# Making the four weight sums of a gate and up block in DRAM, by adding transfers issued from GpSimd

## The chip, the cores and the metric

The kernel runs on one core of one Trainium2 chip. Its five engines work at the same time and wait for each other through semaphores: TensorE (in the profile PE for its matmuls, PEld for its weight loads), VectorE (DVE), ScalarE (ACT), GpSimd (POOL) and SyncE (SP). SP here does nothing but issue transfers (DMAs); ACT issues a few; before the change GpSimd issues none. Each engine takes its instructions strictly in the order of the program, so one that waits holds up all that stand behind it on that engine. The metric is the device time of one execution in microseconds (us); lower is better.

## The reference

One layer of an encoder block on 1024 tokens of width 1024, in float32. The first half makes a convolution group and a neighbourhood attention group and adds their projection to the input. The second half, which the change touches, is a SwiGLU feed-forward network:

```python
h = rms_norm(x, norm2_g[l])
x = x + (jax.nn.silu(h @ w_gate[l]) * (h @ w_up[l])) @ w_down[l]
```

`w_gate` and `w_up` are 1024 x 2816, `w_down` is 2816 x 1024.

## The kernel before

Every float32 operand of a large product is split in two parts, `hi` (a rounded copy, made by ACT) and `lo` (the operand minus `hi`, made by DVE or GpSimd); `mac` (lines 115 to 118) then issues three matmuls, hi by hi, hi by lo and lo by hi. So each operand costs one ACT copy and one subtraction before TensorE may use it.

The core goes through these stages: input projections with the convolution beside them (to about 230 us of the span), attention (to about 340), output projection and second norm (to about 397), gate and up products (to about 800), down projection (to the end).

The gate and up product uses a scheme with seven products instead of eight. The 2816 columns of the two weights are 22 blocks `i` of 128 columns (`FB = 22`). For each block the 1024 rows are two halves, and with gate and up that gives four quadrants: `b11` and `b21` are the two halves of gate, `b12` and `b22` those of up, each 512 rows by 128 columns, 256 KB. Products `m1`, `m2` and `m3` need `b11`, `b21` and `b22` as they are. Products `m5`, `m6`, `m7` and `m4` need four sums T1 to T4 of quadrants. In the kernel before, `load_gu` (line 1071) loads a block in two transfers of 512 KB on SP into two of the four `R` buffers, and `t_sums` (line 1089) makes the four sums as differences on DVE, for two of them on GpSimd, into `ts` tiles (`tqa` for the first two blocks):

```python
l, r = ((b12, b11), (b22, lr(tsum[i, 0])[0]), (b22, b12), (b21, lr(tsum[i, 0])[1]))[n - 1]
(pool if (i, n) in ON_POOL else dve).tensor_tensor(o, l, r, OP.subtract)
```

The other side of each product is a sum of token blocks: `left` (line 1258) makes S1 to S4 from the normed activations `xT` on DVE. `evac` (line 1340) combines the accumulators of the seven products.

For blocks from 4 (`m1`) and 6 (`m2`) on, `m1` and `m2` are themselves done for two blocks at a time by the same scheme one level down (`part`, `prep_part`; tiles `q...`, `qa`, `qb`, `qc`, `qd`, `qs`), with loads of their own (`qr`).

The order is written out by hand. `products` is the list of the products in TensorE's order; `tasks` is the list of the operand preparations, each with a place some products ahead; `prep` takes tasks from it, splits (mostly on ACT and GpSimd) and asks for the next load. R buffers come free when the splits that read them are done. In the first half, `step` (line 468) is called once after each group of matmuls (some 5.5 us) and holds the vector work beside them; the four attention heads' rows are normalised by `score_norm` on GpSimd (line 764) before TensorE turns them (`flip`, line 775).

Names used below: `z` the accumulators of the input projections, `p` the turned attention rows, `e` the exponentials, `cs` a channel sum of the convolution made on GpSimd (line 359), `u` the convolution's channels, `pj` the output projection, `w01r` and the like raw weight chunks loaded on SP (line 150), `tf` the tables for the attention bias built in DRAM by many small transfers, `A`, `B` and `D` the accumulators of the gate and up products.

Of the kernel before, what the change touches and what calls it, by code (L numbers as in the profile page):

```python
# [12 lines left out]
P = 128  # L13
# [18 lines left out]
def layout(v):  # L32
    f = {k: np.asarray(a)[0] for k, a in v.items()}
    w_in = f["w_in"]
    ag = w_in[:, :2 * DC].reshape(KB, P, 8, P).transpose(2, 1, 0, 3)
    qkv = w_in[:, 2 * DC:].reshape(4, 2, P, 3, 512).transpose(3, 0, 2, 1, 4)
    gu = np.stack([f["w_gate"], f["w_up"]]).reshape(2, KB, P, FB, P).transpose(3, 0, 2, 1, 4)
# [12 lines left out]
    out = {  # L50
        "x": f["x"],
        "xp": f["x"].reshape(2, 8, 4, 16, D).transpose(4, 0, 2, 3, 1).reshape(KB, P, S),
        "xt": xt,
        "xa": np.concatenate([xt[0, 0, :, 0, :256], f["norm1_g"][:2 * P].reshape(2, P).T], axis=1),
        "ag": ag.reshape(8, P, KB * P),
        "qkv": qkv.reshape(3, 4, P, 1024),
        "wo": f["w_out"],
        "gu": gu.reshape(FB, 2, P, KB * P),
        "wd": wd,
        "rpb": f["rpb"],  # L60
        "par": par,
    }
    return {k: np.ascontiguousarray(a) for k, a in out.items()}
# [8 lines left out]
def build(ctx, tc, a):  # L72
# [201 lines left out]
    for _ in range(9):  # L274
# [5 lines left out]
    tf = {(rh, ty): dr.tile([16, 8, NH, AR[rh] * NCOL[ty]], F32, name=f"tf{rh}{ty}")  # L280
          for rh in range(2) for ty in range(3)}

    def rstd_of(ss, scale, name):
# [179 lines left out]
        nc.scalar.dma_start(vd[t * P:(t + 1) * P, :], vs)  # L463


    pend = []
# [576 lines left out]
    def square(m, h, eng=pool):  # L1043
# [4 lines left out]
        else:  # L1048
            eng.tensor_tensor(ssum[h], ssum[h], sq, OP.add)  # L1049

    def token_sums(h):
# [11 lines left out]

    def norm2(k, h):
        w = xT[k][:, h * 512:(h + 1) * 512]
        dve.scalar_tensor_tensor(w, w, g2[:, k:k + 1], rows[h], OP.mult, OP.mult)

    HK, QF = KB // 2, FB // 2
    raw_gu, top, tsum = {}, {}, {}

    def load_gu(i, j):
        if i < FB:
            raw_gu[i, j] = R(f"gu{i}{j}")
            nc.sync.dma_start(raw_gu[i, j], a["gu"][ms[i], j])
# [8 lines left out]
    ON_POOL = {("S3", 2), ("S3", 3), ("A22", 1), ("S4", 3), (3, 2), (3, 4),  # L1083
               (0, "m4"), (0, "m5"), (1, "m4"), (1, "m6")}
    ON_DVE = {(3, "m3"), (3, "m7")}

    def t_sums(i, ns):
        (b11, b21), (b12, b22) = lr(raw_gu[i, 0]), lr(raw_gu[i, 1])
        for n in ns:
            if n in (1, 3):  # L1090
                if i > 1:
                    tsum[i, n // 2] = G(f"ts{i}{n}")
                else:
                    tsum[i, n // 2] = tq_slot("tqa", 2 * i + n // 2)
            o = lr(tsum[i, (n - 1) // 2])[(n - 1) % 2]
            l, r = ((b12, b11), (b22, lr(tsum[i, 0])[0]), (b22, b12), (b21, lr(tsum[i, 0])[1]))[n - 1]
            (pool if (i, n) in ON_POOL else dve).tensor_tensor(o, l, r, OP.subtract)  # L1097


    ORDER = ("m1", "m6", "m7", "m2", "m5", "m4", "m3")  # L1100
    ms = [m + h * QF for m in range(QF) for h in range(2)]
# [23 lines left out]
    tasks.sort(key=lambda w: w[0])  # L1125
    quad, raw4, sum4 = {}, {}, {}

    def prep_part(m, i, p):
        j, o = (m, i), 512 * (m == "m2")
        if p == "load":  # L1130
            raw4[j] = G(f"qr{i}{m}")
            for b in range(2):
                nc.sync.dma_start(raw4[j][:, b * 512:(b + 1) * 512], a["gu"][ms[i + b], 0][:, o:o + 512])
            return
        w = raw4[j]
        w11, w12, w21, w22 = [w[:, o:o + 256] for o in range(0, 1024, 256)]
# [87 lines left out]
    def prep(n=1, upto=None):  # L1224
        while tasks and (n > 0 if upto is None else tasks[0][0] <= upto):
            n -= 1
            job = tasks.pop(0)[1]
            if len(job) == 3:
                prep_part(*job)
                continue  # L1230
            i, p = job
            if i > 1 and p in ("m6", "m7"):
                t_sums(i, (1, 2) if p == "m6" else (3, 4))
            b = {"m1": (0, 0), "m2": (0, 1), "m3": (1, 1)}.get(p)
            m = {"m5": 0, "m6": 1, "m7": 2, "m4": 3}.get(p)
            src = lr(raw_gu[i, b[0]])[b[1]] if b else lr(tsum[i, m // 2])[m % 2]
# [5 lines left out]
            split(*top[i, p], src, (dve,) if on_dve else (pool,))  # L1242
            if p == ("m7" if i in (2, 3) or parted(i, "m2") else "m2"):
                load_gu(i + 2, 0)
            if p == "m3":
                load_gu(i + 2, 1)


    sop = {}
# [5 lines left out]
    def left(n, k, what):  # L1255
        sub = pool if (n, k) in ON_POOL else dve
        if n not in sop:
            q = H(n, F32R).rearrange("p (w k s) -> p w k s", w=2, s=512)
            sop[n] = [[q[:, h, i] for i in range(HK)] for h in range(2)]
        o, l, r, op = {"S3": ("21", "11", "21", OP.subtract), "A22": ("22", "22", "22", None),  # L1260
                       "S2": ("22", "22", "21", OP.subtract), "S1": ("21", "22", "11", OP.add),
                       "S4": ("22", "12", "22", OP.subtract)}[n]
        if op is not None and "sum" in what:
# [17 lines left out]
        norm2(k, 0)  # L1281
        split(h2[0][:, k], h2[1][:, k], xT[k][:, :512])

    for i, j in ((0, 0), (0, 1), (1, 0), (1, 1)):
        load_gu(i, j)

    units = [(m, 0) for m in range(4, KB)] + [(m, 1) for m in range(KB)]
    for m in range(4):
        square(m, 0)
    beside = {(1, 1): [lambda: token_sums(0)], (1, 3): [lambda: token_rows(0)],  # L1290
              (0, 1): [lambda: t_sums(0, (1, 2))], (0, 3): [lambda: t_sums(0, (3, 4))],
              (2, 1): [lambda: t_sums(1, (1, 2))], (3, 1): [lambda: t_sums(1, (3, 4))]}
# [39 lines left out]

    def gate2(i, acc):
        dve.tensor_tensor(acc, acc, u2[i], OP.add)  # L1334
        act.activation(acc, acc, AF.Silu)  # L1335

    def up2(i, r, acc):
        dve.tensor_tensor(r, acc, r, OP.mult)
# [2 lines left out]
    def evac(i, p, acc):  # L1341
# [4 lines left out]
            act.copy(l, acc)  # L1346
        elif p == "m6":
            u2[i] = ST(f"u2{i}")
            dve.tensor_tensor(u2[i], acc, l, OP.add)
            if i < 2:  # L1350
                gate2(i, bank[i, "D"])
        elif p == "m2":
# [2 lines left out]
                dve.tensor_tensor(acc, acc, l, OP.add)  # L1355
            act.activation(sl[i], acc, AF.Silu)
        elif p in ("m5", "m7"):
            dve.tensor_tensor(r, acc, l if p == "m7" else r, OP.add)  # L1358
            if i < 2 and p == "m5":
                up2(i, r, bank[i, "D"])  # L1360
        elif p == "m3":
            dve.tensor_tensor(l, acc, l, OP.add)
# [115 lines left out]
    for n, (i, p) in enumerate(products):  # L1478
# [114 lines left out]

# [13 lines left out]
```

## Time and profile before

| | |
|---|---|
| median of 3 runs | 1024.64 us (1024.58 to 1025.29) |
| the profiled execution | 1025.28 us |
| its span, first to last instruction | 1023.6 us |
| granted TensorE clock | 1.000 |
| PE busy | 1017.4 us, 99% of the span |
| PEld busy | 850.2 us, 83% |
| DVE busy | 775.4 us, 76% |
| ACT busy | 480.9 us, 47% |
| POOL busy | 461.6 us, 45% |
| DMA | 151.70 MB in 75756 packets, mean 148 GB/s |

The profile has a page (busy time of each engine, the chain of work that ended last, the costliest groups of instructions, the DMA issues) and views of the trace: groups by line, waits, the timeline, and sums over chosen windows of the span. A row of a group reads: line, engine, operation, tiles written and read, shapes, count, busy time and mean time of one in ns, idle time of the engine before them and who ended it. An engine with a q is its sequencer, which waits or issues. Matmuls are pipelined: two that follow each other overlap in the records, so a busy PE says that it never lacked work, and the time between two starts is what one costs.

### The profile page before, as it was taken

To read this page: it belongs to the slowest core of one execution; us is meant where nothing else is said; L and a number is where in the kernel's file an instruction comes from. 1 tells how busy PE (TensorE), PEld (TensorE's weight loads), DVE (VectorE), ACT (ScalarE), POOL (GpSimd) and SP (SyncE) were. 2 spreads that over 40 slices of the span, in tenths; PEclk is the share of its full clock that TensorE was granted. 3 is DMA by queue.
4 is the path that set the end of the run, shared out by engine and by line. 5 is a ranking of instruction groups with operands and counts; after the bars stand their busy time and mean duration, and the time that the engine had idled before them with its cause. 6 is when DMAs were issued, how large, how long until landed. Compare 5 with 4: busy or idle time off the path is not lost.

```text
span 1023.6 us, 15128 instructions
## 1 busy us (share of the span) xinstructions
PE 1017.4 (99%) x5274; PEld 850.2 (83%) x5274; DVE 775.4 (76%) x1217; ACT 480.9 (47%) x1043; POOL 461.6 (45%) x389
## 2 busy tenths in 40 slices
PE   9999999999999999999999999999999999999998
PEld 8888888877788888888888888888888888888887
DVE  5788897896767474987787787787777766758875
ACT  7556357837878345523434343343332443433432
POOL 1036675535662356167767567567565200003200
PEclk9999999999999999999999999999999999999999
DMA  9426682236503621134334434443341696633631
GB/s 350 168 50 220 202 238 86 101 109 217 165 22 124 247 83 41 45 111 142 132 100 152 155 112 140 139 142 135 120 149 63 237 373 232 216 103 124 221 118 42
DMA packets 75756, 151.70 MB, mean 148 GB/s; under 512 B 14472, under 2 KB 23560, under 8 KB 75040
## 3 DMA queue, kind: packets, MB, share of 16 engines
q1 hardware_dynamic: 73664, 147.38, 42.7%
q10 hardware_dynamic: 2016, 3.36, 0.9%
q8 instruction: 42, 0.69, 0.3%
q14 instruction: 34, 0.28, 0.1%
HBM read 112.06 MB, written 44.11 MB: 153 GB/s over the span
## 4 chain that ended last, share of the span: by engine, by line
PE 94%; DVE 2%; ACT 2%; issue 1%; POOL 1%; DVEq 0%; POOLq 0%; ACTq 0%
PE B L116 5%; PE B L117 5%; PE B L118 5%; PE z L116 4%; PE z L118 4%; PE z L117 4%; PE D L116 4%; PE D L117 4%; PE D L118 4%; PE gl L118 3%; PE gl L117 3%; PE gl L116 3%; PE pj L116 2%; PE pj L118 2%; PE pj L117 2%; PE p L775 2%
## 5 line engine op out<-in xcount | busy, mean ns | idle before, releaser
L378 DVE SCALAR_TENSOR_TENSOR cv<-u,par,cv 128x1009 f32<-128x1009 f32 (+14 forms) x92 | 117.5, 1277 | 2.3
L1550 POOL TENSOR_TENSOR ou<-ou,resm 128x512 f32<-128x512 f32 x8 | 12.7, 1602 | 139.3 <-DVE ou L1541 126.1
L405 POOL TENSOR_TENSOR pa<-pa,pr 128x1022 f32<-128x1022 f32 (+5 forms) x24 | 58.0, 2416 | 37.3 <-ACT pr L404 33.3
L108 ACT CAST op<-sr 128x512 fp32r<-128x512 f32 x77 | 47.6, 619 | 57.5 <-PE B2d L118 26.8
L112 DVE TENSOR_TENSOR op<-sr,op 128x512 fp32r<-128x512 f32 x77 | 57.2, 742 | 17.2 <-ACT op L108 17.2
L108 ACT CAST op<-wd 128x512 fp32r<-128x512 f32 x54 | 33.4, 619 | 29.0 <-DVE wd L1445 18.1
L753 ACT ACTIVATE e<-e,mx 128x341 f32<-128x341 f32 (+5 forms) x64 | 35.3, 553 | 18.1 <-DVE mx L748 18.1
L1097 DVE TENSOR_TENSOR ts<-gu,ts 128x512 f32<-128x512 f32 x38 | 42.9, 1129 | 0.7
L764 POOL TENSOR_SCALAR e<-e,rs 128x341 f32<-128x341 f32 (+5 forms) x64 | 32.9, 528 | 22.1 <-DVE rs L762 21.6
L112 DVE TENSOR_TENSOR op<-wd,op 128x512 fp32r<-128x512 f32 x54 | 38.9, 721 | 1.7 <-ACT op L108 0.5
L748 DVE CUSTOM_DVE_ANT_0 e<-s,tab 128x341 f32<-128x341 f32 (+5 forms) x64 | 27.2, 481 | 13.1 <-PE s L731 12.9
L1049 POOL TENSOR_TENSOR sq<-sq,sq 128x512 f32<-128x512 f32 x12 | 17.0, 1418 | 41.7 <-ACT sq L1045 41.5
L1358 DVE TENSOR_TENSOR g<-D,g 128x512 f32<-128x512 f32 x22 | 15.2, 689 | 23.4 <-PE D L118 23.4
L432 ACT ACTIVATE sq<-z,r 128x64 f32<-128x64 f32 x96 | 28.2, 326 | 4.3 <-PE z L118 4.3
L1335 ACT ACTIVATE D<-D 128x512 f32<-128x512 f32 x22 | 12.8, 582 | 33.2 <-DVE D L1334 33.2
L404 ACT ACTIVATE pr<-u,par 128x1022 f32<-128x1022 f32 (+5 forms) x24 | 27.0, 1138 | 1.6 <-ACT vs L462 1.6
L116 PE MATMUL B2d<-op 128*128 128x512 f32 x66 | 25.8, 391 | 0.0
L118 PE MATMUL B2d<-op 128*128 128x512 f32 x66 | 25.7, 389 | 0.0
L117 PE MATMUL B2d<-op 128*128 128x512 f32 x66 | 25.7, 389 | 0.0
L775 PEld LDWEIGHTS p<-ident,e 128*128 128x128 f32 (+1 forms) x184 | 19.7, 135 | 6.7 <-POOL e L764 5.1
L936 DVE TENSOR_TENSOR xT<-pj,xT 128x512 f32<-128x512 f32 x16 | 10.8, 686 | 19.0 <-PE pj L118 18.8
L775 PE MATMUL p<-ident,e 128*128 128x128 f32 (+1 forms) x184 | 23.9, 277 | 0.0
(1478 smaller groups left out, 3766.2 us busy)
## 6 DMA issues: line engine op xcount, KB each, us to landing
gu<-in_gu SPq DMA_DIRECT2D x44, 512.0 KB
sr<-sd SPq DMA_DIRECT2D x77, 256.0 KB
sd<-sd SPq DMA_DIRECT2D x22, 512.0 KB
wd<-in_wd SPq DMA_DIRECT2D x36, 256.0 KB
sd<-g SPq DMA_DIRECT2D x33, 256.0 KB
x<-in_x SPq DMA_DIRECT2D x8, 512.0 KB
xT<-in_xp SPq DMA_DIRECT2D x8, 512.0 KB
xd<-xT SPq DMA_DIRECT2D x16, 256.0 KB
```

Source lines behind the costliest of these rows:

```text
L108: act.copy(hi, src)
L112: eng.tensor_tensor(*[w[..., sl] for w in (lo, src, hi.bitcast(F32))], OP.subtract)
L116: pe.matmul(acc, lh, rh, start=start, stop=False, skip_group_check=True)
L117: pe.matmul(acc, lh, rl, start=False, stop=False, skip_group_check=True)
L118: pe.matmul(acc, ll, rh, start=False, stop=stop, skip_group_check=True)
L378: dve.scalar_tensor_tensor(acc[:, o], uc[:, i], dwk[:, c, t:t + 1], acc[:, o], OP.mult, OP.add)
L405: pool.tensor_tensor(pa[:, o], pa[:, o], pr[:, o], OP.add)
L432: act.activation(sq[:, h * HD:(h + 1) * HD], z[:, h * HD:(h + 1) * HD], AF.Square, scale=r, accum_out=ss[:, h:h + 1])
L753: act.activation(e, e, AF.Exp, bias=mx.pop((i, hh)), scale=-1.0, accum_out=sums[i][:, hh:hh + 1])
L764: pool.tensor_scalar(es[i][:, hh], es[i][:, hh], rs[:, hh:hh + 1], 1.0, op0=OP.mult, op1=OP.mult)
L775: pe.transpose(pt[:m, g * P:(g + 1) * P], et[i][:, hh, k.start:k.start + m], ident)
L1097: (pool if (i, n) in ON_POOL else dve).tensor_tensor(o, l, r, OP.subtract)
```

## The change

The quadrants are laid out so that each is 32 rows of 8 KB in DRAM. For each of the 22 blocks SP copies the whole block (1 MB) from the input to a DRAM tile `td` (`copy_in`). Then four transfers issued from GpSimd, with addition, make T1, T3, T2 and T4 in place in `td` (`add_in`): T1 = b11 + b12, T3 = b12 + b22, T2 = b22 + T1, T4 = b21 + T2. That is 88 adding transfers of 256 KB. `load_gu` loads one operand of 256 KB at a time, from the input or from `td`, two of them into one R buffer, after every second split; before it loads a sum whose additions have not been issued it issues them.

Since an adding transfer can only add, the sums replace the former differences, and signs are moved to the token side: the second half of the tokens' second half of rows is normed with -g (`ng2`), `S1`, `S2` and `S3` change accordingly, `evac` subtracts where it added, and one `Silu` gets scale -1.

`add_in` is called from `step` (from its 3rd call on, between the 9th and the 21st on every other call only), after each unit of the output projection, and after every second product of the gate and up stage from the 16th on. Of the 88 additions, 30 stand in the stages before the attention loop, 12 in the output projection, 46 in the gate and up stage. The `ts` and `tqa` tiles and `t_sums` are gone; the pool of small tiles `sm` has 11 buffers instead of 12, and the scratch for GpSimd's transfer descriptors is 128 bytes of each partition instead of 64. The matmuls are the same, in the same order.

```diff
+    gu = np.stack([f["w_gate"], f["w_up"]]).reshape(2, 2, KB // 2, P, FB, P).transpose(4, 1, 0, 3, 2, 5)
+    gu = gu.reshape(FB, 4, P, 512)[:, [0, 1, 3, 2]]
...
-        return T("sm", [P, 8], 12, name)[:, :n]
+        return T("sm", [P, 8], 11, name)[:, :n]
...
+    QUAD = {"b11": 0, "b12": 1, "b22": 2, "b21": 3, "T1": 0, "T3": 1, "T2": 2, "T4": 3}
+    td = [dr.tile([P, 2048], F32, name=f"td{i}") for i in range(FB)]
+
+    def quadrant(i, q):
+        w = td[i] if q[0] == "T" else a["gu"][ms[i]]
+        return w[QUAD[q] * 32:QUAD[q] * 32 + 32]
+
+    def copy_in(i):
+        if i < FB:
+            nc.sync.dma_start(td[i], a["gu"][ms[i]])
+
+    adds = [(i, *q) for i0 in range(0, FB, 2) for q in (("T1", "b12"), ("T3", "b22"), ("T2", "T1"), ("T4", "T2"))
+            for i in (i0, i0 + 1)]
+
+    def add_in(n=1):
+        for _ in range(n):
+            if adds:
+                i, o, w = adds.pop(0)
+                if o == "T4":
+                    copy_in(i + 4)
+                nc.gpsimd.dma_start(quadrant(i, o), quadrant(i, w), accum_op=OP.add, max_dma_last_dim=8192)
...
+    ADD_AT = (3, 9, 21)
...
         behind()
+        n_step[0] += 1
+        if ADD_AT[0] <= n_step[0] and not (ADD_AT[1] <= n_step[0] < ADD_AT[2] and n_step[0] % 2):
+            add_in()
...
+    for i in range(4):
+        copy_in(i)
     take(1)
     r_rows(0)
...
+        g = ng2[:, k - 4:k - 3] if h and k > 3 else g2[:, k:k + 1]
+        dve.scalar_tensor_tensor(w, w, g, rows[h], OP.mult, OP.mult)
...
+    def load_gu():
+        if n_load[0] < len(halves):
+            w = R(f"gu{n_load[0]}")
+            for h in range(2):
+                i, p = ip = halves[n_load[0]]
+                while any((i, FACTOR[p]) == w[:2] for w in adds):
+                    add_in()
+                raw_gu[ip] = lr(w)[h]
+                nc.sync.dma_start(raw_gu[ip], quadrant(i, FACTOR[p]).rearrange("r (a m) -> (r a) m", a=4))
+                n_load[0] += 1
...
-            if i > 1 and p in ("m6", "m7"):
-                t_sums(i, (1, 2) if p == "m6" else (3, 4))
...
+            split(*top[i, p], raw_gu.pop((i, p)), (dve,) if on_dve else (pool,))
+            n_split[0] += 1
+            if n_split[0] % 2 == 0:
+                load_gu()
...
+        if n == "S2" and "sum" in what:
+            dve.scalar_tensor_tensor(block(o, k), block(l, k), -1.0, block(r, k), OP.mult, OP.subtract)
...
         proj(m, h, part_)
         unravel()
+        add_in()
...
-            dve.tensor_tensor(u2[i], acc, l, OP.add)
+            dve.tensor_tensor(u2[i], acc, l, OP.subtract)
...
+        if n > 15 and n % 2 == 0:
+            add_in()
...
-    nc = bacc.Bacc("TRN2", target_bir_lowering=False, num_devices=1, dynamic_dma_scratch_size=64)
+    nc = bacc.Bacc("TRN2", target_bir_lowering=False, num_devices=1, dynamic_dma_scratch_size=128)
```

More of the change, by code (lines that the diff above doesn't have):

```diff
@@ L281, in build @@
           for rh in range(2) for ty in range(3)}
+    QF = FB // 2
+    ms = [m + h * QF for m in range(QF) for h in range(2)]
+    QUAD = {"b11": 0, "b12": 1, "b22": 2, "b21": 3, "T1": 0, "T3": 1, "T2": 2, "T4": 3}
[15 more added lines that the diff above has]
+                nc.gpsimd.dma_start(quadrant(i, o), quadrant(i, w), accum_op=OP.add, max_dma_last_dim=8192)
     def rstd_of(ss, scale, name):
@@ L1049, in square @@
             eng.tensor_tensor(ssum[h], ssum[h], sq, OP.add)
+    ng2 = g1[:, :4]
+    dve.tensor_scalar(ng2, g2[:, 4:], -1.0, None, op0=OP.mult)
     def token_sums(h):
@@ L1065, in norm2 @@
         w = xT[k][:, h * 512:(h + 1) * 512]
[L1066 to L1074, printed above, removed]
+        g = ng2[:, k - 4:k - 3] if h and k > 3 else g2[:, k:k + 1]
+        dve.scalar_tensor_tensor(w, w, g, rows[h], OP.mult, OP.mult)
+    HK = KB // 2
+    top, raw_gu, n_split, n_load = {}, {}, [0], [0]
+    FACTOR = {"m1": "b11", "m2": "b21", "m3": "b22", "m4": "T4", "m5": "T1", "m6": "T2", "m7": "T3"}
+    def load_gu():
[8 more added lines that the diff above has]
+                n_load[0] += 1
     tqs = {}
@@ L1081, in tq_slot @@
         return tqs[name][:, q * 1024:(q + 1) * 1024]
-    ON_POOL = {("S3", 2), ("S3", 3), ("A22", 1), ("S4", 3), (3, 2), (3, 4),
+    ON_POOL = {("S3", 2), ("S3", 3), ("A22", 1), ("S4", 3),
                (0, "m4"), (0, "m5"), (1, "m4"), (1, "m6")}
     ON_DVE = {(3, "m3"), (3, "m7")}
[L1087 to L1097, printed above, removed]
     ORDER = ("m1", "m6", "m7", "m2", "m5", "m4", "m3")
-    ms = [m + h * QF for m in range(QF) for h in range(2)]
     products = [(i, p) for i0 in (0, 2) for p in ("m1", "m2") for i in (i0, i0 + 1)]
@@ L1125, in build @@
     tasks.sort(key=lambda w: w[0])
+    halves = [job for _, job in tasks if len(job) == 2]
     quad, raw4, sum4 = {}, {}, {}
     def prep_part(m, i, p):
-        j, o = (m, i), 512 * (m == "m2")
+        j = (m, i)
         if p == "load":
@@ L1132, in prep_part @@
             for b in range(2):
-                nc.sync.dma_start(raw4[j][:, b * 512:(b + 1) * 512], a["gu"][ms[i + b], 0][:, o:o + 512])
+                src = quadrant(i + b, "b11" if m == "m1" else "b21").rearrange("r (a m) -> (r a) m", a=4)
+                nc.sync.dma_start(raw4[j][:, b * 512:(b + 1) * 512], src)
             return
@@ L1259, in left @@
             sop[n] = [[q[:, h, i] for i in range(HK)] for h in range(2)]
-        o, l, r, op = {"S3": ("21", "11", "21", OP.subtract), "A22": ("22", "22", "22", None),
-                       "S2": ("22", "22", "21", OP.subtract), "S1": ("21", "22", "11", OP.add),
+        o, l, r, op = {"S3": ("21", "21", "11", OP.subtract), "A22": ("22", "22", "22", None),
+                       "S2": ("22", "22", "21", OP.subtract), "S1": ("21", "11", "22", OP.subtract),
                        "S4": ("22", "12", "22", OP.subtract)}[n]
-        if op is not None and "sum" in what:
+        if n == "S2" and "sum" in what:
+            dve.scalar_tensor_tensor(block(o, k), block(l, k), -1.0, block(r, k), OP.mult, OP.subtract)
+        elif op is not None and "sum" in what:
             dve.tensor_tensor(block(o, k), block(l, k), block(r, k), op)
@@ L1282, in h2_one @@
         split(h2[0][:, k], h2[1][:, k], xT[k][:, :512])
-    for i, j in ((0, 0), (0, 1), (1, 0), (1, 1)):
-        load_gu(i, j)
+    for _ in range(4):
+        load_gu()
     units = [(m, 0) for m in range(4, KB)] + [(m, 1) for m in range(KB)]
@@ L1357, in evac @@
         elif p in ("m5", "m7"):
-            dve.tensor_tensor(r, acc, l if p == "m7" else r, OP.add)
+            dve.tensor_tensor(r, acc, l if p == "m7" else r, OP.subtract if p == "m7" else OP.add)
             if i < 2 and p == "m5":
```

20 lines of the change are left out of this document (5 added, 15 removed).

## The prediction

> **What bounds the kernel now.** I read the page's head and chain first, then sums over the stages, then TensorE's waits.
>
> ```profile
> span 1023.6 us, 15128 instructions
> ...
> PE 1017.4 (99%) x5274; PEld 850.2 (83%) x5274; DVE 775.4 (76%) x1217; ACT 480.9 (47%) x1043; POOL 461.6 (45%) x389
> ...
> PE 94%; DVE 2%; ACT 2%; issue 1%; POOL 1%; DVEq 0%; POOLq 0%; ACTq 0%
> ```
>
> TensorE is busy in 99% of the span and carries 94% of the chain that ended last. By stage (window, its length, then busy us and count of PE, PEld, DVE, ACT, POOL, the granted clock, DMA share, GB/s):
>
> ```profile
> 0.00:230.00 230.00, 228.94 (x1043) 188.84 (x1045) 191.11 (x231) 134.21 (x350) 103.97 (x56) 1.00 0.52 169
> 230.00:340.00 110.00, 109.00 (x894) 86.20 (x893) 77.58 (x217) 86.29 (x216) 56.58 (x115) 1.00 0.45 146
> 340.00:440.00 100.00, 100.00 (x454) 82.84 (x453) 65.77 (x101) 43.43 (x75) 44.45 (x33) 1.00 0.25 90
> 440.00:525.00 85.00, 84.07 (x421) 70.91 (x420) 67.51 (x96) 30.14 (x57) 60.61 (x45) 1.00 0.34 123
> 525.00:800.00 275.00, 275.00 (x1493) 239.18 (x1492) 214.83 (x340) 98.53 (x189) 175.40 (x131) 1.00 0.38 129
> 800.00:1024.00 224.00, 220.43 (x977) 182.24 (x975) 158.60 (x237) 88.32 (x157) 20.55 (x14) 1.00 0.55 187
> ```
>
> The gate and up stage runs from about 397 to 800. TensorE is idle there for 85.00 - 84.07 = 0.93 us, all of it between 440 and 525; from 340 to 440 and from 525 to 800 it is never idle, and its clock is full. TensorE's waits between 340 and 800:
>
> ```profile
> PE q41m L118 <- POOL qb4m L112: 0.5, 1, 0.5
> PE D L116 <- DVE g L1338: 0.4, 1, 0.4
> ```
>
> So the work that the change takes away lies beside a TensorE that is full, and the change leaves the 5274 matmuls as they are. What it can win is in these two waits. What it can lose is anywhere.
>
> **What it removes from DVE and GpSimd.** 86 subtractions leave DVE and two leave GpSimd. Those of blocks 2 to 21, 78 on DVE:
>
> ```profile
> L1097 DVE TENSOR_TENSOR ts<-gu,ts 128x512 f32<-128x512 f32 x38 | 42.9, 1129 | 0.7
> L1097 DVE TENSOR_TENSOR ts<-gu 128x512 f32<-128x512 f32 x20 | 15.5, 777 | 0.0
> L1097 DVE TENSOR_TENSOR ts<-gu,gu 128x512 f32<-128x512 f32 x20 | 15.5, 774 | 0.0
> ```
>
> 42.9 + 15.5 + 15.5 = 73.9 us, and 8 more for the first two blocks at about 0.8 us, 6 us. Some 80 us of DVE go, and TensorE waited for DVE for 0.4 us in the whole stage. The worth of it is read where TensorE stops (GpSimd and one ACT row around the two waits):
>
> ```profile
> 454.86 0.68 DVE L1097 TENSOR_TENSOR ts<-gu,gu 128x512 f32<-128x512 f32 x1
> 455.00 1.68 POOL L112 TENSOR_TENSOR qb4m<-qs4m,qb4m 128x512 fp32r<-128x512 f32 x1 [5.63 <-DVE qs4m L1145]
> ...
> 462.06 1.30 POOL L1097 TENSOR_TENSOR ts<-gu,ts 128x512 f32<-128x512 f32 x1
> 462.36 0.63 ACT L108 CAST qc4m<-qs4m 128x512 fp32r<-128x512 f32 x1
> 463.32 1.30 POOL L112 TENSOR_TENSOR qc4m<-qs4m,qc4m 128x512 fp32r<-128x512 f32 x1
> 464.58 1.73 POOL L112 TENSOR_TENSOR t3m<-ts,t3m 128x512 fp32r<-128x512 f32 x1
> 464.67 0.19 PEld L118 LDWEIGHTS q42m<-qT3m,qc4m 128*128 128x128 f32 x1 [0.20 <-POOL qc4m L112]
> ```
>
> The first wait is for `qb4m`, which took 1.68 us with a `ts` of DVE beside it; `qc4m`, the same form, takes 1.30. Without that `ts` it is 0.38 us earlier. For `qc4m` TensorE's load waits 0.20 us; it starts behind a `ts` of GpSimd at 463.32, though ACT's half is there at 462.36 + 0.63 = 462.99. With the `ts` gone those 0.20 us go too, unless the addition issued there takes its place. The wait for `g` L1338 I leave as it is: DVE has its other work in front of it. Gain: 0.38 + 0.20 = 0.6 us, between 0 and 0.93. What is late next is TensorE itself. The sign changes (4 two-input sums on DVE become one form with a scalar, one tiny multiplication for -g) replace like by like, hidden by the same TensorE.
>
> **What it adds to SP.** 44 loads of 512 KB become 120 of 256 KB and 22 copies of 1 MB come: 98 issues more.
>
> ```profile
> L1074 SPq DMA_DIRECT2D gu<-in_gu x44: 327/332/1096, 338.8 to 768.4; - x44
> ...
> SPq L1074 <- DVE ts L1097: 125.5, 17, 9.8
> ```
>
> 98 x 0.33 = 33 us of issuing over 770 us, hidden, since these loads spend 125.5 us waiting for `ts` to give back its R buffer, and that wait goes. In its place SP waits for GpSimd's splits and for additions to land. Loads are asked for six products ahead, some 20 us, and a load behind a late addition takes the `g` stores queued behind it along; I price that at nothing because 20 us of lead cover it.
>
> **What it adds to GpSimd.** 88 issues. No row shows a transfer issued from GpSimd, so its price c is bounded from both sides: from below by SP's 0.33 us for a `gu` load above, from above by GpSimd's own longest operation, 2.4 us:
>
> ```profile
> 229.39 2.39 POOL L359 TENSOR_TENSOR cs<-cs,u 128x1024 f32<-128x1024 f32 x1 [14.02 <-DVE rs L762]
> 231.75 0.94 POOL L764 TENSOR_SCALAR e<-e,rs 128x253 f32<-128x253 f32 x2
> ...
> 233.21 0.60 PE L775 MATMUL p<-ident,e 128*128 128x128 f32 x4
> ...
> 60.48 0.95 POOL L523 MEMSET neg<- 128x1024 f32 x1
> ```
>
> I take c = 0.95 us, the row of the MEMSET: like the writing of descriptors it reads nothing and writes something. In the gate and up stage 46 issues cost 44 us; GpSimd has 360 - 60.61 - 175.40 = 124 us free there between 440 and 800, with idle time in front of most splits, and splits run several products ahead. At nothing on the path.
>
> In one place there is no cover. `cs` ends at 231.75 and waits for DVE's last convolution sum; right behind it in the program stand the additions of two calls of `step` (after the seventh `z` of the values, and the bare one before `score_norm(0)`), and then the two normalisations of `e`, which TensorE turns at 233.21. They end at 231.75 + 0.94 = 232.69; the second pair of turns starts at about 233.44, so the slack is 0.75 us. Two issues make it a wait of 2c - 0.75: 1.15 us at c = 0.95, nothing at 0.33, 4.1 us at 2.4. TensorE issues in order and is full behind it, so this is lost for good. The other 28 early additions fall where GpSimd idles for a ScalarE half or for DVE (the 14.02 us before `cs` are an example).
>
> **What it adds to the DMA engines.** 22 MB copied, 22 MB added, and 30 MB of loads where 22 were. In the gate and up stage, at a share of 0.38 and less, there is room. The dense stretch is earlier:
>
> ```profile
> 110.00:160.00 50.00, 50.00 (x224) 41.41 (x223) 45.10 (x40) 19.90 (x41) 33.68 (x15) 1.00 0.87 253
> 160.00:210.00 50.00, 50.00 (x235) 41.34 (x235) 40.27 (x41) 41.32 (x145) 30.74 (x14) 1.00 0.19 70
> ...
> ACT w0q L108 <- DMA w01r<-in_qkv: 8.0, 1, 8.0
> ```
>
> There 253 GB/s x 50 us = 12.7 MB move; about five additions and two copies, some 3.3 MB, come on top: 0.87 x 1.26 = 1.10, an excess of 5 us of transfers that the next window, at 0.19, takes up. TensorE is never idle in it although ACT waits 8.0 us for a weight chunk. At nothing.
>
> **The sum.** The profiled execution is 1025.28 us (span 1023.6). 1025.28 + 1.15 - 0.6 = 1025.8. It is 0.64 above the median of the runs, 1024.64, so the forecast for a median is 1025.2. The bounds of the two terms alone: 1024.64 - 0.93 = 1023.7 (c small, both waits gone) and 1024.64 + 4.1 = 1028.7 (c = 2.4, nothing gained).
>
> **Rivals.**
>
> *The second of the two additions has to wait for the first (slower).* The descriptor scratch is small; the diff itself doubles it to 128 bytes. If it holds one addition of 32 rows but not two, GpSimd stands in the second issue until the first has been carried out. For: two issues back to back occur just here, in front of `score_norm(0)`. Against: nothing in the trace shows such a ring. The price of a transfer from issue to use, from a busy stretch: 126.56 - 122.18 = 4.4 us.
>
> ```profile
> 122.18 0.53 SPq L150 DMA_DIRECT2D w01r<-in_qkv  x1
> ...
> 126.56 1.05 ACT L108 CAST w0q<-w01r 128x1024 fp32r<-128x1024 f32 x1 [7.98 <-DMA w01r<-in_qkv]
> ```
>
> 1.15 + 4.4 - 0.6 = 4.95 us: 1029.6. It decides from a wait of about 1.5 us on.
>
> The Trainium skill, "DMA: Bandwidth & Descriptors", section "Anatomy of one DMA", speaks against the change at this point: it gives a transfer issued from GpSimd a fixed cost of about 2.0 us beside its bytes, most of it the confirmation that the last byte has landed. By its formula 256 KB take an estimated 2.6 us, and the rival would come to 1.15 + 2.6 - 0.6 = 3.15 us, 1027.8. No run shown here has such a transfer.
>
> *GpSimd gets too full in the gate and up stage (slower).* It decides from c = 124 / 46 = 2.7 us on. At c = 3.0 it lacks 46 x 0.3 = 14 us, and the wait at 233 is 5.3: 1044. Splits that come late one by one, with c near 2.4, give less, 1027 to 1032. For: each issue stands in front of splits that TensorE uses. Against: 175.40 busy of 275.00 us.
>
> *The early transfers crowd each other (slower).* ACT already waits 8.0 us for `w01r`; if the excess of 5 us lands on it and TensorE runs out of filled accumulators, up to 5 us: 1025 to 1030.
>
> *Faster.* c near 0.33 and all of TensorE's idle time in the stage gone: 1023.7, which is still within 0.2%. Beyond that something else would have to speed TensorE up, and no row shows what.
>
> **How the numbers follow.** A measurement of this kernel tells 0.2%, 2.05 us, from no change. Forecast, the two terms cancelling within 2 us of 1024.64: 0.52. Full scratch 0.22, full GpSimd 0.12, crowding 0.08: slower 0.42. Faster by more than 0.2%: 0.06. The likeliest case has the range 1023.7 to 1026.7. The range for 8 in 10 takes in the full scratch with c at 1.3 (2 x 1.3 - 0.75 + 4.4 = 6.3, 1030.9) and leaves out a full GpSimd and a large gain: 1023.3 to 1031.0.
>
> **What would show it.** Right: PE busy unchanged, `ts` gone from DVE, about 80 us less DVE time, a new wait of PE for POOL `e` L764 of about 1 us near 233, the wait for `qb4m` shorter, no new one between 525 and 800. The full scratch: that wait at 3 us or more, with GpSimd standing in its second issue. Wrong: PE idle between 525 and 800 (splits or loads late), or before 230 (transfers).

## The result, and the profile after

The change makes the kernel slower: 1059.89 us in the median (1053.8 to 1062.6) against 1024.87 of the kernel before on the same chip, a ratio of 1.0333 (95% interval 1.0288 to 1.0378). The profiled execution took 1059.86 us, with a span 34.5 us longer than before. The page of the kernel after, its head and its chain:

```profile
span 1058.1 us, 15426 instructions
...
PE 1025.5 (97%) x5274; PEld 854.2 (81%) x5274; DVE 749.7 (71%) x1132; ACT 475.6 (45%) x1043; POOL 504.3 (48%) x475
...
PE 68%; issue 11%; POOL 10%; DMA 4%; SPq 3%; ACT 2%; DVE 1%; POOLq 0%; DVEq 0%; ACTq 0%
```

The matmuls are the same 5274. What changed is the chain: TensorE carried 94% of it and now carries 68%; the rest went to "issue", GpSimd, DMA and SP's queue. The sums by stage say where (window, its length, then busy us and count of PE, PEld, DVE, ACT and POOL, granted clock, DMA share, GB/s):

```profile
0.00:230.00 230.00, 221.84 (x1001) 182.24 (x1001) 182.40 (x215) 131.60 (x343) 117.35 (x77) 0.99 0.81 239
230.00:340.00 110.00, 103.00 (x860) 79.99 (x859) 71.63 (x215) 72.76 (x204) 63.22 (x121) 0.97 0.51 145
340.00:440.00 100.00, 86.24 (x376) 70.23 (x375) 55.81 (x56) 41.22 (x64) 45.10 (x40) 0.93 0.70 200
440.00:525.00 85.00, 84.92 (x394) 70.81 (x394) 66.56 (x104) 32.76 (x60) 42.08 (x34) 1.00 0.49 140
525.00:800.00 275.00, 274.87 (x1499) 239.22 (x1498) 197.25 (x278) 99.30 (x199) 196.37 (x175) 1.00 0.74 207
```

TensorE is idle 8.2 us before 230 (1.1 in the kernel before), 7.0 from 230 to 340 (1.0), 13.8 from 340 to 440 (0.0), and 0.2 from 440 to 800 (0.9). That is 26 us more. The stage for which the change was made, gate and up from 440 on, loses nothing; the loss lies ahead of it, in three places. TensorE's waits name them:

```profile
PE ss L1088 <- DVE sq L1080: 13.5, 2, 12.4
PE p L806 <- POOL e L795: 6.3, 1, 6.3
PE z L118 <- POOL w03l L113: 2.3, 1, 2.3
PE z L118 <- POOL w02l L113: 1.9, 1, 1.9
```

They stand at 143 to 154 us (`w02`, `w03`), at 242 to 249 (`e`) and at 417 to 429 (`ss`). Some 8 us more are slower matmuls (PE busy 1025.5 us against 1017.4 for the same matmuls): the clock falls in just these stages. The 8 us behind the last of the stalls in a view of their own:

```profile
429.48:433.50 4.02, 4.02 (x14) 3.54 (x15) 0.18 (x1) 0.27 (x1) 2.97 (x3) 0.50 0.95 234
433.50:437.50 4.00, 4.00 (x17) 3.20 (x16) 1.61 (x3) 2.07 (x3) 2.83 (x3) 0.77 0.61 166
```

At a granted clock of 0.50 a matmul of 512 columns takes 0.43 us from start to start instead of 0.23. The Trainium skill, "TensorE: Matmul & The Clock Gate", Part 1, states such a gate: half rate after an idle window of some 3.4 us, and again some 3.4 us of work until full rate. The trace agrees that the clock halves behind a stall, but the half rate lasts longer here: 0.50 for 4.02 us and 0.77 in the mean of the next 4.00 make some 5.9 us (an estimate from these two rows; 5.5 us behind the stall at 242 by the same working). At the first place the clock halves behind two gaps of 1.7 and 1.9 us with a single matmul between them.

**The wait at 242.** GpSimd and TensorE in the timeline of the kernel after (start, duration, instruction, in brackets the idle time before it and who ended it):

```profile
237.90 0.81 POOL L306 DMA_DIRECT2D td<-in_gu  x1 [1.13 <-issue]
...
242.99 0.79 POOL L306 DMA_DIRECT2D td<-in_gu  x1 [1.82 <-issue]
247.53 0.78 POOL L306 DMA_DIRECT2D td<-in_gu  x1 [3.75 <-issue]
248.07 1.21 POOL L795 TENSOR_SCALAR e<-e,rs 128x253 f32<-128x253 f32 x2
...
248.89 1.14 PE L806 MATMUL p<-ident,e 128*128 128x128 f32 x4 [6.30 <-POOL e L795]
```

GpSimd stands in front of both additions. They start 5.1 and 4.5 us after the one before. The view of the line gives the same for all 88:

```profile
L306 POOL DMA_DIRECT2D td<-in_gu x44: 552/790/1071, 38.2 to 776.4; - x44
L306 POOL DMA_DIRECT2D td<-td x44: 746/794/1308, 67.1 to 797.2; - x44
...
  issue: 82.5, 31
...
DMA to landing us min/median/max: 3.8/5.0/10.5
```

An addition costs 0.79 us of record (the next instruction starts some 0.55 us after its start), lands 5.0 us after its issue in the median, and GpSimd stands in front of 31 of them for 82.5 us in all. That fits a scratch that can have one addition on the way and not two; the first experiment tests it.

**The wait at 417.** The last steps in front of `ss`, and DVE some 25 us earlier, in the same timeline:

```profile
393.54 4.03 POOL L113 TENSOR_TENSOR h<-xT,h 128x512 fp32r<-128x512 f32 x3
...
393.88 10.11 DVE L113 TENSOR_TENSOR t0m<-gu,t0m 128x512 fp32r<-128x512 f32 x1 [1.27 <-ACT t0m L109]
...
397.26 1.05 POOL L306 DMA_DIRECT2D td<-td  x1
...
416.12 0.79 POOL L306 DMA_DIRECT2D td<-td  x1 [1.66 <-issue]
...
425.48 0.78 POOL L306 DMA_DIRECT2D td<-in_gu  x1 [6.06 <-DMA xd<-xT]
426.05 1.51 POOL L1080 TENSOR_TENSOR sq<-sq,sq 128x512 f32<-128x512 f32 x1
...
427.59 1.74 DVE L1080 TENSOR_TENSOR sq<-sq,sq 128x512 f32<-128x512 f32 x1 [7.02 <-POOL sq L1080]
...
429.48 0.77 PE L1088 MATMUL ss<-one,sq 128*128 128x1 f32 x3 [12.44 <-DVE sq L1080]
```

Two things meet. GpSimd had stood in front of additions from 375 on, so from 391.8 to 405 it works off a backlog without a gap, and in that stretch one split on DVE, a form of 0.69 us, takes 10.11 us; all that stands behind it on DVE is late. Then the addition of 416.12, which lands only after 9.1 us, at 425.2, holds the next one until 425.48 (the profile puts this wait down to `xd`), and the square sum behind it is what `ss` waits for. Which of the two is worth how much here was not measured apart; the larger scratch below bears on it.

**The waits at 143 to 154.** SP and ACT:

```profile
131.48 0.53 SPq L151 DMA_DIRECT2D w01r<-in_qkv  x1
...
135.20 1.05 ACT L109 CAST w0q<-w01r 128x1024 fp32r<-128x1024 f32 x1 [12.90 <-DMA w01r<-in_qkv]
```

The chunk arrives no slower than before: 3.7 us from issue to use, where it was 126.56 - 122.18 = 4.4. It is asked for 9.3 us later (131.48 against 122.18), because SP is late. The next chunk, `w02r`, for which TensorE itself waits, is asked for 8.3 us later (139.76 against 131.42) and takes 1.3 us longer to its use (5.2 against 3.9). SP's own waits between 60 and 142 us, the two longest beside the one for `zero`:

```profile
SPq L570 <- DMA t<-neg: 3.2, 1, 3.2
SPq L570 <- DMA td<-in_gu: 1.8, 1, 1.8
```

Without that wait, 33.1 us in the kernel before and 28.7 after, SP waits 9.6 us in this stretch (1.8 in the kernel before), and it issues two copies of 0.55 us more.

### The profile page after: what moved, and what is told of

It is laid out like the page before. It is cut to its first block, busy times and chain, and to the rows that moved or that the text cites. A ratio compares the mean times of both kernels' runs of the same rounds, so it can differ in the third digit from the quotient of the medians.

```text
span 1058.1 us, 15426 instructions
## 1 busy us (share of the span) xinstructions
PE 1025.5 (97%) x5274; PEld 854.2 (81%) x5274; DVE 749.7 (71%) x1132; ACT 475.6 (45%) x1043; POOL 504.3 (48%) x475
## 4 chain that ended last, share of the span: by engine, by line
PE 68%; issue 11%; POOL 10%; DMA 4%; SPq 3%; ACT 2%; DVE 1%; POOLq 0%; DVEq 0%; ACTq 0%
PE B L117 5%; PE B L118 5%; PE B L119 5%; PE D L117 3%; PE D L118 3%; PE D L119 3%; POOL pa L430 3%; PE p L806 2%; PE o L829 2%; PE s L762 2%; POOL td L306 1%; PE B2d L117 1%; PE z L117 1%; PE B2d L118 1%; PE z L119 1%
## 5 line engine op out<-in xcount | busy, mean ns | idle before, releaser
L1578 POOL TENSOR_TENSOR ou<-ou,resm 128x512 f32<-128x512 f32 x8 | 12.4, 1559 | 140.5 <-DVE ou L1569 127.2
L306 POOL DMA_DIRECT2D td<-in_gu x44 | 35.8, 814 | 87.6 <-issue 51.7
L430 POOL TENSOR_TENSOR pa<-pa,pr 128x1022 f32<-128x1022 f32 (+5 forms) x24 | 62.0, 2583 | 13.8 <-ACT pr L429 7.4
L306 POOL DMA_DIRECT2D td<-td x44 | 36.8, 837 | 49.7 <-issue 30.8
L1384 DVE TENSOR_TENSOR g<-B,g 128x512 f32<-128x512 f32 x22 | 15.2, 689 | 25.3 <-PE B L119 25.3
L1388 DVE TENSOR_TENSOR g<-B,g 128x512 f32<-128x512 f32 x22 | 15.1, 685 | 19.1 <-PE B L119 19.0
L1252 ACT ACTIVATE sl<-sl 128x512 f32<-128x512 f32 x16 | 9.3, 582 | 39.7 <-DVE sl L1251 39.7
```

Of the source, the lines that this page charges most:

```text
L306: nc.gpsimd.dma_start(quadrant(i, o), quadrant(i, w), accum_op=OP.add, max_dma_last_dim=8192)
L430: pool.tensor_tensor(pa[:, o], pa[:, o], pr[:, o], OP.add)
L1384: dve.tensor_tensor(r, acc, l if p == "m7" else r, OP.subtract if p == "m7" else OP.add)
```

## The experiments

Stated first: the scratch for descriptors holds one addition, so GpSimd stands (theory 1); the rivals were that GpSimd stands for another reason, and that the transfers as such make things late.

**A larger scratch alone.** The small tiles pay for it.

```diff
-        return T("sm", [P, 8], 11, name)[:, :n]
+        return T("sm", [P, 8], 7, name)[:, :n]
...
-dynamic_dma_scratch_size=128
+dynamic_dma_scratch_size=256
```

> The kernel after with one number changed: a descriptor scratch of 256 bytes of each partition instead of 128 (paid with 7 small tiles instead of 11). If the scratch is what holds GpSimd (it holds one addition and not two), the 82.5 us in which GpSimd stands in front of additions fall below 15 us, TensorE's wait for the normalised `e` falls from 6.3 to about 0.9 us (two issues at 0.8 less 0.75 of slack), the wait for `ss` falls from 12.4 to under 3 us, and the loss at 140 to 155 stays, since GpSimd did not stand there: 1059.9 - 5.4 - 10 to 13 and the slower matmuls behind both stalls, 1036 to 1044 us. If GpSimd stands for another reason (additions that wait for each other, or the DMA engines being full), the 82.5 us stay and the time is 1055 to 1062.

Measured 1038.87 us (ratio 1.013, 1.0113 to 1.0147), 21 us less than the kernel after. The view of the line has no "issue" in front of additions any more, although each takes longer to land (the row was 3.8/5.0/10.5):

```profile
  DMA td<-in_gu: 7.7, 2
...
DMA to landing us min/median/max: 3.9/6.0/10.4
```

The wait for `ss` is gone. That for `p` is 2.3 us instead of 6.3, and not the 0.9 expected: two issues in a row still stand in front of `e`, and DVE waits 3.9 us there for GpSimd's normalisation, probably for a small tile, of which there are four fewer. The waits for `w02` and `w03` stay. DVE's `t0m` still takes 5.31 us, and yet TensorE doesn't wait for `ss`: a DVE instruction of that length does not by itself make `ss` late. Theory 1 holds for the second and third place, and not for the first.

**Each place by itself.** Three edits to the kernel after, each taking the additions away from one place:

```diff
-    ADD_AT = (3, 9, 21)
+    ADD_AT = (21, 9, 21)
```

> The kernel after without the 12 additions of steps 3 to 20; the queue of additions starts at step 21 and all stand 12 places later, the last ones behind each other in front of the loads that need them. If the additions' traffic makes the weights late at 140 to 155, the waits for `w02l` and `w03l` and the 8 us of loss there go, and ACT waits for `w01r` 8 us again instead of 12.9; the other two stalls stay: about 1051 us. If the copies of 1 MB (which stay) are the cause, that place keeps 5 us or more of its loss: 1056 to 1060.

```diff
-        if ADD_AT[0] <= n_step[0] and not
+        if n_step[0] not in (35, 36) and ADD_AT[0] <= n_step[0] and not
```

> The kernel after without the additions of the two calls of step in front of the first normalisation (steps 35 and 36); all later ones move two places back. Both theories of the wait (full scratch, or only the two issues) say that TensorE's wait of 6.3 us for `e` near 242 falls below 1 us. If the loss there (8.5 us with the slower matmuls behind it) comes from this wait alone, the time falls by 6 to 9 us to 1051 to 1054, with the other two places as they are; if GpSimd's backlog from the additions before them is enough, 2 to 5 us of the wait stay.

```diff
         unravel()
-        add_in()
```

> The kernel after without the additions behind the units of the output projection; the 12 additions move into the gate and up stage, the last ones in front of the loads that need them. If GpSimd's standing in these units and the backlog behind it make the second half of the square sums late, TensorE's wait of 12.4 us for `ss` goes and DVE's split `t0m`, 10.1 us in the kernel after, takes 2 us or less: 1059.9 - 13 = 1047 us, or a little more if additions forced late in the gate and up stage cost there. If the transfers themselves (loads of `gu` from the DRAM tiles) make it late, the wait stays at 8 us or more.

Each removed its place, or most of it: with the first, whose copies stay, `w01r` is asked for at 120.65 and TensorE is busy in all of the 50 us from 110 to 160; with the second TensorE no longer waits for GpSimd's `e`, though 2.0 us are left there for ACT's `e`; with the third there is no wait for `ss` and `t0m` takes 0.88 us in the mean. The second took 1056.33 us, one execution, where 1051 to 1054 were expected: four sums, two more than in the kernel after, had to be issued in front of loads of blocks 18 and 20, and TensorE waits 4.1 and 1.7 us for splits behind them. Its wait for `ss` fell too, to 5.8 us at the longest, so this run does not price the place alone. But the first took 1090.6 us and the third 1100.35, one execution each, where 1051 and 1047 were expected. Their additions moved into the gate and up stage, where from block 12 on `load_gu` found sums not yet issued and issued them, one or two at a time, in front of splits. New waits of TensorE in the first:

```profile
PE q140m L119 <- POOL qa14m L113: 6.0, 2, 4.0
...
PE q200m L119 <- POOL qa20m L113: 4.3, 1, 4.3
```

GpSimd stands 124.8 us in front of additions there (120.9 in the third). So the early places bought something: the gate and up stage can issue 7 additions in 14 products and needs 8, and lives on the stock made ahead.

**Everything but the additions.** The copies, the half-size loads and the signs stay. This kernel leaves out the four sums: its products take unsummed quadrants.

```diff
-                nc.gpsimd.dma_start(quadrant(i, o), quadrant(i, w), accum_op=OP.add, max_dma_last_dim=8192)
```

> The kernel after without the 88 additions; the copies into the DRAM tiles, the loads of 256 KB and the signs stay (so the four sums are left out, and the products that need them take unsummed quadrants). If the copies alone make the weights late at 140 to 155 (one is issued at 109.8 us), TensorE still loses about 8 us there: 1033 us. If the additions' traffic (256 KB read twice and written once for each, five of them between 105 and 154 us) is what tips it, nothing is lost anywhere: 1024 to 1026 us, which also prices everything in the change but the additions.

1023.37 us (one execution; the lowest of the kernel before on this chip was 1024.43). Nothing is lost at 140 to 155: `w01r` is asked for at 123.21, 1.0 us later than before, not 9.3. And of the gate and up waits none is left; from 440 to 525 TensorE is idle 0.07 us:

```profile
440.00:525.00 85.00, 84.93 (x428) 72.38 (x427) 52.12 (x85) 28.20 (x55) 55.84 (x42) 1.00 0.53 183
```

So everything but the additions is worth some 1.6 us (by this one execution), and the 88 additions cost 36. They also take back most of DVE's relief: DVE is busy for 688.2 us here and for 749.7 in the kernel after, with the same work.

**Why DVE's split took 10 us.** First bursts of work for GpSimd in the kernel before, where it has none:

```diff
+                for _ in range(12):
+                    pool.tensor_tensor(om["m1"][:, :512], quarter(om["m1"], 2048, 0), quarter(om["m1"], 2048, 0), OP.add)
...
+                for _ in range(12):
+                    pool.memset(om["m1"][:, :1024], 0.0)
```

> The kernel before with work added for GpSimd in the down projection, where it has none and DVE works through splits with two inputs in SBUF one after the other: first 12 additions of 128x512 behind each other (about 15 us, from about 837 us), later (from about 868 us) 12 MEMSETs of 128x1024 behind each other (about 11 us), which read nothing. If GpSimd's reading instructions, when they follow each other without a gap, keep DVE's instructions with two SBUF inputs out for their whole length (the explanation for `t0m`, 10.1 us instead of 0.69 in the kernel after), then DVE has instructions of 5 to 15 us beside the additions and none over 0.8 beside the MEMSETs. If the two take turns, no DVE instruction takes over 2.1 us (one of GpSimd's 1.3 and its own 0.7) and GpSimd's own stretch instead; the 10.1 us then has another cause. TensorE may lose some us in the first case, nothing in the second.

The timeline of this kernel (1025.53 us, one execution), GpSimd's two bursts and DVE beside each:

```profile
836.74 16.94 POOL L1535 TENSOR_TENSOR om<-om 128x512 f32<-128x512 f32 x12 [36.01 <-DVE om L1532]
...
846.91 1.52 DVE L112 TENSOR_TENSOR op<-sr,op 128x512 fp32r<-128x512 f32 x1
...
869.31 12.10 POOL L1541 MEMSET om<- 128x1024 f32 x12
...
872.89 0.69 DVE L112 TENSOR_TENSOR op<-sr,op 128x512 fp32r<-128x512 f32 x1
```

They take turns, 1.52 us for each DVE instruction; beside the MEMSETs DVE is not held up. The Trainium skill, "SBUF — State Buffer", section "Who interferes with whom", has this rule: a DVE instruction with two SBUF inputs contends with GpSimd instructions that read SBUF, not with those that only write it. The trace agrees (1.52 against 0.69). But turns do not make 10 us, so my first explanation, back-to-back reading instructions, fell. The next kernel, made from the kernel after, has the burst twice (into four slots in turn), the second time behind one adding transfer:

```diff
+                for n in range(12):
+                    pool.tensor_tensor(om["m1"][:, n % 4 * 512:n % 4 * 512 + 512], quarter(om["m1"], 2048, 0), quarter(om["m1"], 2048, 0), OP.add)
...
+                nc.gpsimd.dma_start(quadrant(0, "T1"), quadrant(0, "b12"), accum_op=OP.add, max_dma_last_dim=8192)
...
```

> The kernel after with two equal bursts of 12 additions of 128x512 for GpSimd in the down projection, each into four slots in turn; the second burst has one adding transfer (256 KB, between DRAM tiles no longer needed) issued in front of it. In the kernel before with such a burst, DVE and GpSimd took turns: DVE's instructions with two SBUF inputs took 1.52 us each, none longer. If the issue of a transfer is what lets GpSimd's next instructions queue up so closely that DVE gets no turn (in the kernel after, GpSimd's splits behind an addition stand 1.25 us apart with records of 1.54), the first burst shows DVE at 1.5 us and the second one DVE instruction of 10 to 16 us. If the different output slots are what matters (the burst before wrote one slot), both bursts show long ones. If neither, both show 1.5 us and the 10.1 us of `t0m` stays open.

```profile
872.46 16.82 POOL L1563 TENSOR_TENSOR om<-om 128x512 f32<-128x512 f32 x12 [37.09 <-DVE om L1560]
...
888.31 1.52 DVE L113 TENSOR_TENSOR op<-wd,op 128x512 fp32r<-128x512 f32 x1
...
904.80 0.78 POOL L1568 DMA_DIRECT2D td<-in_gu  x1
...
905.33 12.78 DVE L113 TENSOR_TENSOR op<-sr,op 128x512 fp32r<-128x512 f32 x1
905.37 12.18 POOL L1570 TENSOR_TENSOR om<-om 128x512 f32<-128x512 f32 x12
```

Behind the issue GpSimd needs 12.18 us for what took 16.82, and DVE gets no turn until the burst is over. The run took 1070.83 us (one execution), and TensorE waits 6.1 us for this split. With a drain of GpSimd between the transfer and the burst:

```diff
+                nc.gpsimd.drain()
```

> The kernel with the two bursts and the transfer in front of the second, with one instruction more: GpSimd's drain between the transfer and the burst, so that the instructions behind an issue start only when GpSimd is done with what stands in front of them. If DVE gets no turn because GpSimd's instructions behind an issue are queued closer than they end (in that kernel one DVE instruction took 12.78 us beside 12 additions 1.01 us apart), the drain ends this: DVE's instructions take 1.5 us in the second burst as in the first. If the issue leaves something else behind (descriptors still written or the transfer in flight), one DVE instruction again takes 5 us or more.

```profile
907.07 0.79 POOL L1568 DMA_DIRECT2D td<-in_gu  x1
912.57 17.07 POOL L1571 TENSOR_TENSOR om<-om 128x512 f32<-128x512 f32 x12 [4.72 <-issue]
...
912.75 1.53 DVE L113 TENSOR_TENSOR op<-sr,op 128x512 fp32r<-128x512 f32 x1
```

The turns are back (1.53 us; the run 1065.68 us, one execution, with a wait of 0.7 us in place of the 6.1), but the drain holds GpSimd for 4.72 us, until the transfer has landed (5.3 us after its issue at 907.07). So in these bursts it is the issue that changes the order of access for the instructions that follow it without a gap. Why the hardware does so no run here shows. It outlasts the transfer: the one in the kernel without the drain landed 5.5 us after its issue, and DVE stayed out for 12.78.

**Putting the additions elsewhere.** The scratch of 192 or 256 bytes (9 or 7 small tiles), no additions before step 21 nor in steps 35 and 36, and three for four products later, so that none is left to be issued in front of a load:

```diff
-    ADD_AT = (3, 9, 21)
+    ADD_AT = (21, 9, 21)
...
-        if ADD_AT[0] <= n_step[0] and not
+        if n_step[0] not in (35, 36) and ADD_AT[0] <= n_step[0] and not
...
-        if n > 15 and n % 2 == 0:
+        if n > 15 and n % 4 != 3:
```

> The kernel after with 192 bytes of scratch (9 small tiles instead of 11), no additions before step 21 nor in steps 35 and 36, and three additions for four products instead of two from the 16th product on, so that none is left to be issued in front of a load. If the three places account for the whole loss and nothing new is late, 1024 to 1027 us with PE idle no more than 2 us above the kernel before. If the 192 bytes (two additions at once) are still too few, GpSimd stands 10 us or more in front of additions and a part of the wait for `ss` stays: 1030 to 1040.

> As the kernel with 192 bytes, but with 256 bytes and 7 small tiles. Nothing stands in front of additions: 1024 to 1027 us if the small tiles do not hold up the score maxima; 2 us more near 235 if they do (in the kernel after with 256 bytes alone DVE waited 3.9 us there for GpSimd to give back a small tile). If it is under 1023.8, the change pays where its transfers are placed otherwise.

1034.91 us (1.0109, 1.009 to 1.0128) and 1035.68 (1.0103, 1.0088 to 1.0118), some 8 us over the top of what was expected. The first falls into its second range, 1030 to 1040, by luck: GpSimd does stand 16.0 us in front of additions with 192 bytes, but not at all for room with 256, and the times are alike. The three places are mended, and a fourth is new. From the kernel with 192 bytes, TensorE's longest wait, and SP:

```profile
PE o L829 <- DMA vw<-vd: 4.5, 1, 4.5
```

```profile
239.40 1.15 SPq L295 DMA_DIRECT2D td<-in_gu  x2
241.14 9.85 SPq L709 DMA_DIRECT2D vw<-vd  x8
```

With later additions the two copies that go with the second pair's T4 are asked for at 239, in front of the loads of the attention's value rows; eight of those took 2.97 us before. Hence the last placing, with 192 bytes and early additions in steps 21 to 34 alone:

```diff
-        if n_step[0] not in (35, 36) and ADD_AT[0] <= n_step[0] and not
+        if n_step[0] < 35 and ADD_AT[0] <= n_step[0] and not
```

> As the kernel with 192 bytes, 9 small tiles and three additions for four products, but with the early additions in steps 21 to 34 alone: none in the four steps around the first normalisation, so that the copies of the second pair of blocks (two of 1 MB at 239 us in that kernel, in SP's queue in front of the loads of `vw`, which then took 9.85 us instead of 2.97) are issued in the output projection. If those copies were its whole remaining loss (offset against the kernel before growing from 0 to 9.2 us between 240 and 249 us and not later), the time is 1024 to 1026 us, and the wait of `o` for `vw` is gone. If GpSimd's larger load later on costs more, 1027 to 1035. Under 1023 the change pays with this placing; everything but the additions ran at 1023.4.

1028.24 us (1.0029, 1.0018 to 1.0039): the wait for `vw` is gone, and it is the best placing found, still slower than before. What is left is DVE kept out, now in the gate and up stage:

```profile
538.13 0.78 POOL L306 DMA_DIRECT2D td<-td  x1
...
540.00 6.04 DVE L1413 TENSOR_TENSOR sd<-g,sd 128x512 f32<-128x512 f32 x1
...
546.07 0.62 ACT L109 CAST t8m<-gu 128x512 fp32r<-128x512 f32 x1 [4.01 <-DVE sd L1413]
```

```profile
PE B L117 <- ACT t8m L109: 1.5, 1, 1.5
PE D L117 <- DVE g L1384: 1.5, 1, 1.5
```

The second wait stands behind a DVE split of 7.3 us at 466. A drain behind each addition was tried as a cure:

```diff
+                nc.gpsimd.drain()
```

> The kernel at 1028.24 us (192 bytes, early additions in steps 21 to 34 alone, three for four products) with a drain of GpSimd behind each addition. If its remaining loss (TensorE 1.5 us for `g` near 472 and 1.5 us for `t8m` near 544, behind DVE instructions of 7.3 and 6.0 us) is DVE kept out by GpSimd, DVE's longest instructions with two inputs fall to about 2 us, these two waits go, and the time is 1024 to 1025.5. If a drain costs more than 0.3 us or waits until the transfer has been carried out (about 5 us each), GpSimd gets late instead: 1030 us or more.

1290.02 us (1.2585, 1.2561 to 1.261): the second branch of the expectation. The drain waits for the transfer, up to 7.2 us of GpSimd behind an issue. As a test of the cause it came out as the first branch said: the longest 128x512 sum or difference of two tiles on DVE takes 2.47 us, as without any addition (2.47) and in the kernel before (2.51); without the drain it takes 7.26, and in the kernel after 10.11.

## Why the prediction was wrong

The forecast of 1025.2 us is 35 us too low and outside its range. Point by point:

- *"What it removes".* Right in kind: with everything but the additions the waits for `qb4m` and `qc4m` are gone, and the gain is 1.6 us in one execution for the 0.6 taken (bounds 0 to 0.93); 0.86 of it is idle time of TensorE from 440 to 525, inside the bounds, and where the rest lies stays open. The sign of "about 80 us less DVE time" did not come: DVE has 25.7 us less, since the additions made its instructions longer.
- *The price c of an issue, 0.95 us.* Near: 0.79 of record, 0.55 until the next instruction starts.
- *The place before `score_norm(0)`.* The place was right, the forecast's size of 1.15 was not; the rival "second addition waits for the first" was. Its formula with c = 0.95 gives a wait of 2 x 0.95 - 0.75 + 4.4 = 5.55 us; measured were 6.3. The landing of 4.4 us taken from a load's row is close to the measured 5.0. The estimate of 2.6 us from the formula of the Trainium skill, "DMA: Bandwidth & Descriptors", section "Anatomy of one DMA", is half of what an addition takes here, and the measurement decides. The sign that the prediction gave for it, GpSimd standing in the second issue, came too. The rival was too unlikely at 0.22, and its price was set for one place only: a scratch that holds one addition holds up GpSimd wherever two stand within 5 us of each other, in 31 of 88 cases.
- *"The other 28 early additions fall where GpSimd idles".* This is the step that failed most. It did not name the output projection, where 12 additions stand behind units of 24 matmuls, 5.4 us at 0.227, hardly longer than a landing. There GpSimd's standing, its backlog and DVE's 10.11 us end in the wait of 12.4 us for `ss`, the largest single loss.
- *"What it adds to SP: hidden".* It counted the gate and up loads and 20 us of lead, and not the first stage, where SP is in order and the weights are queued behind small transfers that wait for each other. With the additions these land later, SP waits 7.8 us more, and the chunk comes 9.3 us later. The early transfers cost the first stage 7 us of TensorE, the loss that the third rival named (up to 5 us), but by another way: the late chunk was asked for late and did not travel slowly.
- *"GpSimd gets too full in the gate and up stage".* Not in the kernel after, idle 0.2 us from 440 to 800. It came true in the two kernels with 12 additions moved into that stage, through standing and not through c.
- *The sum.* Each of the three places also costs a half-rate stretch, some 8 us in all. The prediction had no term for that.

Not foreseen by any rival: DVE kept out behind an issue.

## What to carry to other kernels

A transfer issued from GpSimd has two prices: the issue (0.8 us), and the time until the scratch has room for the next (5 us with room for one); place such transfers further apart than a landing, or pay for the scratch first. Read the whole in-order queue that a new transfer joins or slows, SP's above all, in the busiest stage of the kernel, and not in the stage for which the change was made. When an engine that has slack gets new work, look at who shares a resource with it: here the relief of DVE, 87 us without the additions, shrank to 26 with them, and single DVE instructions took 6 to 10 us.

## What the runs showed of the hardware that was not expected

- Behind a transfer issued by GpSimd, gapless GpSimd instructions with SBUF inputs keep a DVE instruction with two SBUF inputs out for their whole length: 12.78 us against turns of 1.52 us without the transfer, and 1.53 with a drain between.
- GpSimd's drain waits for its transfer: 4.72 us behind an issue of 0.79, with the transfer landing after 5.3.
- An adding transfer of 256 KB between DRAM tiles lands after 3.8 to 10.5 us, 5.0 in the median with one on the way; with room for more on the way the median was 6.0.
